# A feed-forward of seven-product block multiplications: from one fused loop to two phases through DRAM

## The chip, the core and the metric

One Trainium2 chip, one of its cores. The metric is device microseconds of one execution, lower is better. Profiles are of one execution each.

## What is computed

One layer of a hybrid decoder on 1024 tokens of width 1024, all in float32:

```python
x = layer_norm(x, emb_ln_g, emb_ln_b)
proj = x @ w_in                      # queries, keys, values, pool input
mixed = concat(stick_breaking_attention, multiscale_pool) @ w_out
x = layer_norm(ALPHA * x + mixed, ln1_g, ln1_b)
h = square(relu(x @ w_up)) @ w_down  # 1024 -> 4096 -> 1024
x = layer_norm(ALPHA * x + h, ln2_g, ln2_b)
x = layer_norm(ALPHA * x + (p @ w_ple) * sigmoid(x @ w_gate), ln3_g, ln3_b)
```

The change is in the feed-forward, the line of `h`, and in what hands its inputs over.

## The kernel before

Float32 products are made of reduced-precision ones: `split` (L59) takes a tile into a rounded part h (a ScalarE copy, L61) and the rest l (a subtraction on VectorE or POOL, L62), and `mm3` (L64 to L67) issues three matmuls, h x h, l x h and h x l, of 128 x 128 stationary by 512 moving columns. All transfers go through one queue, that of SyncE (SP), by `load` (L69), which serves for loads and stores alike.

Tiles come from pools with a fixed number of buffers for each tag (L50: "X" 16, "K" 14, "ra" 6, "at" 4, "VS" 3, "DG" 1, "wr" 2, "wt" 4, of 1024 columns each); PSUM has four tags b0, b2, b4, b6 of two banks each. The framework orders the instructions of each engine by a planned timeline, in which a buffer must be free before its next tile is written. Where a `manual_schedule` names an engine, the instructions of the block keep the order of the code on that engine.

**Up to the feed-forward.** Eight token tiles of 128 are normalised and transposed (`norm0`, L162), attention and pooling run head by head (L515 to L543), their results lie in DRAM (mspill) and the normalised input too (xspill). The output projection (L580 to L607) goes in three rounds of three, three and two token tiles; in each the eight k blocks of w_out are loaded and split, and all six (or four) banks accumulate. Eight tiles xres are loaded from xspill ahead of the first round (L566 to L568). After a round each of its tiles is added (L599), normalised (L601), transposed and split into x1h and x1l (L603 to L607).

**The feed-forward** works on 16 groups of 256 hidden columns. `up` (L635) makes a 128 x 512 block of the hidden values, one of four for a group (two halves of the hidden columns by two halves of the tokens), with 8 x 3 matmuls, then relu on ScalarE (L646) and the square on VectorE (L647). The second product takes the group's hidden values as a 2 x 2 block matrix a, and the group's rows of w_down as a 2 x 2 block matrix b. In place of eight block products it makes seven, p1 to p7, of sums and differences of the blocks (s1 to s4 of a on VectorE, t1 to t4 of b on POOL, L631, L632), each split again; some products are added up in a PSUM bank one after the other and every state of a bank is added to xres by VectorE as it is (`into`, L692, mostly L695). `down` (L708) issues three matmuls for a product and a token tile. The loop at L766 to L777 interleaves the up products of group g + 1 with the down products of group g; the last group is made plainly, with eight block products (`plain`, L727).

**The tail** (L835 to L871) has the orders of TensorE and VectorE, and at first of POOL, written out by hand: plain products, the second layer norm of tile 0 and 1 (`norm2`), then for each token tile the gate product (`gate`, L817, 48 matmuls), its merge and the third norm. The weights of the gate are split into gw ahead of it (L790 to L796).

## Time and profile before

| | us |
|---|---|
| median of 3 runs | 1269.9 (1268.44 to 1271.51) |
| the profiled execution | 1269.56 |
| its span, first to last instruction | 1267.8 |

The engines are PE (TensorE matmuls), PEld (its weight loads, beside them), DVE (VectorE), ACT (ScalarE), POOL (GpSimd) and SP (the queue of transfers). L62 is line 62 of the kernel. Matmuls overlap, so a busy PE is not one at its peak: the distance from start to start counts. "[1.92 <-DVE xres L695]" behind an instruction says that its engine stood idle for 1.92 us before it and that this VectorE instruction ended the wait. PEclk is the clock granted to TensorE, as a share of the full one.

### The profile page before, as it was taken

The page shows a single profiled execution, that of the slowest core. Times are in us where ns is not written, and L with a number is a line of the kernel's source. Part 1 is how long each engine was busy: PE and PEld are TensorE (multiplying, and loading weights), DVE is VectorE, ACT ScalarE, POOL GpSimd, SP SyncE. Part 2 cuts the span into 40 slices and gives each one's busy share as a digit, 9 for nine tenths or more (in the row PEclk, how much of TensorE's full clock was granted, in tenths as well). Part 3 has the DMA queues.
Part 4 walks back from the last instruction along what each step waited for, and adds up shares of the span by engine and source line. Part 5 has one row for each costly group of instructions (what it writes and reads, how often), then busy time and mean ns, then how long its engine had stood idle before and what let it go on. Part 6 is the DMA issues. An engine that isn't in the chain of part 4 may idle for free.

```text
span 1267.8 us, 15286 instructions
## 1 busy us (share of the span) xinstructions
PE 1204.0 (95%) x5700; PEld 997.0 (79%) x5700; DVE 991.3 (78%) x1314; ACT 476.9 (38%) x894; POOL 588.2 (46%) x429
## 2 busy tenths in 40 slices
...
GB/s 349 285 116 117 43 42 58 43 64 53 72 172 215 128 116 133 67 67 17 67 50 67 36 48 67 50 67 17 67 50 67 36 48 67 51 166 17 67 81 69
DMA packets 79802, 108.21 MB, mean 85 GB/s; under 512 B 4592, under 2 KB 59376, under 8 KB 79728
## 3 DMA queue, kind: packets, MB, share of 16 engines
...
## 4 chain that ended last, share of the span: by engine, by line
PE 70%; DVE 11%; issue 4%; POOL 3%; ACT 3%; DMA 2%; DVEq 0%; SPq 0%; POOLq 0%; ACTq 0%
PE pu L66 9%; PE pu L67 9%; PE pu L65 9%; PE pd L65 7%; PE pd L66 7%; PE pd L67 7%; PE pq L65 2%; PE pq L66 2%; PE pq L67 2%; PE tp L115 2%; PE acc L66 2%; PE o L422 2%; DVE xres L106 2%; PE acc L65 2%; PE acc L67 2%
## 5 line engine op out<-in xcount | busy, mean ns | idle before, releaser
L695 DVE TENSOR_TENSOR xres<-xres,pd 128x512 f32<-128x512 f32 x420 | 267.1, 677 | 81.0 <-PE pd L67 81.0
L66 PE MATMUL pu<-x1l,wh 128*128 128x512 f32 x512 | 199.1, 389 | 1.1 <-DVE x1l L62 1.1
L65 PE MATMUL pu<-x1h,wh 128*128 128x512 f32 x512 | 199.1, 389 | 0.9 <-DVE xres L599 0.9
L67 PE MATMUL pu<-x1h,wl 128*128 128x512 f32 x512 | 199.1, 389 | 0.0
L62 POOL TENSOR_TENSOR wl<-wraw,wh 128x1024 fp32r<-128x1024 f32 x43 | 104.7, 2437 | 189.1 <-ACT wh L61 188.3
L62 POOL TENSOR_TENSOR t<-b,t 128x512 fp32r<-128x512 f32 x63 | 86.6, 1375 | 160.4 <-ACT t L61 160.4
L61 ACT CAST wh<-wraw 128x1024 fp32r<-128x1024 f32 x68 | 71.7, 1054 | 189.1 <-PE pu L66 124.6
L66 PEld LDWEIGHTS pu<-x1l,wh 128*128 128x128 f32 x512 | 96.1, 188 | 21.5 <-DVE x1l L62 1.6
L65 PEld LDWEIGHTS pu<-x1h,wh 128*128 128x128 f32 x512 | 96.0, 188 | 21.4 <-ACT x1h L61 1.5
L67 PEld LDWEIGHTS pu<-x1h,wl 128*128 128x128 f32 x512 | 96.1, 188 | 20.4 <-POOL wl L62 0.5
L647 DVE TENSOR_TENSOR a<-a 128x512 f32<-128x512 f32 x64 | 101.8, 1590 | 7.3 <-ACT a L646 7.2
L61 ACT CAST s<-a 128x512 fp32r<-128x512 f32 x62 | 38.4, 621 | 140.6 <-DVE a L632 139.0
L100 POOL TENSOR_TENSOR rs<-var,mhalf 128x1 f32<-128x1 f32 x32 | 44.7, 1400 | 94.5 <-DVE var L98 94.5
L65 PE MATMUL pq<-xh,wh 128*128 128x512 f32 x192 | 78.0, 406 | 0.9 <-DVE ul L62 0.8
L393 DVE TENSOR_TENSOR_SCAN rr<-rr,diag 128x640 f32<-128x640 f32 (+3 forms) x32 | 71.4, 2233 | 8.2 <-ACT rr L391 8.1
L396 POOL TENSOR_TENSOR aa<-aa,rr 128x639 f32<-128x639 f32 (+3 forms) x32 | 57.0, 1781 | 44.8 <-DVE rr L393 44.8
L65 PE MATMUL pd<-t,s 128*128 128x512 f32 x192 | 74.8, 390 | 2.1 <-ACT s L61 2.1
L67 PE MATMUL pq<-xh,wl 128*128 128x512 f32 x192 | 76.7, 400 | 0.0
L62 POOL TENSOR_TENSOR b<-b,b 128x512 fp32r<-128x512 f32 x46 | 72.5, 1603 | 9.1 <-ACT b L61 9.1
L66 PE MATMUL pq<-xl,wh 128*128 128x512 f32 x192 | 76.6, 399 | 0.0
L66 PE MATMUL pd<-t,s 128*128 128x512 f32 x192 | 74.7, 389 | 0.0
L632 POOL TENSOR_TENSOR b<-b,b 128x512 f32<-128x512 f32 x45 | 71.5, 1588 | 6.5 <-DMA b<-in_w_down_dram 1.7
...
## 6 DMA issues: line engine op xcount, KB each, us to landing
b<-in_w_down_dram SPq DMA_DIRECT2D x32, 512.0 KB, 3.5
wraw<-in_w_up_dram SPq DMA_DIRECT2D x32, 512.0 KB, 4.1
wraw<-in_w_out_dram SPq DMA_DIRECT2D x24, 512.0 KB, 3.4
wraw<-in_w_in_dram SPq DMA_DIRECT2D x16, 512.0 KB, 5.2
xt<-in_x_dram SPq DMA_DIRECT2D x8, 512.0 KB, 8.1
pspill<-pe SPq DMA_DIRECT2D x8, 512.0 KB, 5.4
xspill<-xn SPq DMA_DIRECT2D x8, 512.0 KB, 5.5
vspill<-vst SPq DMA_DIRECT2D x8, 512.0 KB, 3.0
```

The lines of the kernel that those rows point to most:

```text
L61: A.copy(out=h, in_=src)
L62: (eng or V).tensor_tensor(out=l, in0=src, in1=h.bitcast(F32), op=ALU.subtract)
L65: T.matmul(ps, lhsT=lh, rhs=rh, start=start, stop=False, **kw)
L66: T.matmul(ps, lhsT=lh, rhs=rl, start=False, stop=False, **kw)
L67: T.matmul(ps, lhsT=ll, rhs=rh, start=False, stop=stop, **kw)
L100: G.tensor_tensor(out=rs, in0=var, in1=mhalf[:, 0:1], op=ALU.pow)
L106: V.scalar_tensor_tensor(out=dst[:, cs], in0=dst[:, cs], scalar=rs, in1=b[:, cs], op0=ALU.mult, op1=ALU.add)
L393: V.tensor_tensor_scan(out=rr[:, 0:n][:, ::-1], data0=rr[:, 0:n][:, ::-1], data1=diag[:, S - n:S][:, ::-1], initial=0.0, op0=ALU.mult, op1 ...
L396: G.tensor_tensor(out=aa[:, 0:n - 1], in0=aa[:, 0:n - 1], in1=rr[:, 1:n], op=ALU.mult)
L632: (V if dst[0] == "a" else G).tensor_tensor(out=value[dst], in0=value[a], in1=value[b], op=op)
L647: V.tensor_tensor(out=rl, in0=rl, in1=rl, op=ALU.mult)
L695: V.tensor_tensor(out=xres[i][:, cs], in0=xres[i][:, cs], in1=src, op=ALU.add)
```

## The change

The seven-product scheme is used for the first product too, and the two products no longer alternate.

- **Phase one** makes the hidden values of all 16 groups. The 2 x 2 blocks are now those of w_up (two halves of 512 input features by the group's two halves of hidden columns, sums on VectorE, `up_first`, `up_rest`) and of the transposed x (two halves of the features by two halves of the tokens, sums t1 to t4 made once, in `second_half` and `x_sums`). A product is 4 x 3 matmuls instead of 8 x 3, and there are seven for a group instead of four. Relu and square are both on ScalarE. VectorE then makes the sums s1 to s4 for the second product, and four tiles `hid` go to DRAM (hspill, seven blocks of 512 columns a group). `down_sums` loads the rows of w_down, POOL makes their four sums in place, and four stores bring them to DRAM (tspill).
- **Phase two** takes two groups a step, in eight steps. `down_operands` reloads the blocks in four stages j (hidden values, side 0, split with VectorE; the blocks of w_down and its sums, side 1, split with POOL), and `down` adds the two groups' products (2 x 3 matmuls) in a bank before `into` takes it.
- Tag "X" has 8 buffers of twice the width (`big`). The normalised x goes to DRAM (rspill) and comes back as xres ahead of phase two; in the output projection three tiles xr are loaded ahead and one more as each is done.
- The tail's hand-written order has the last step's products, and gw 4 to 7 are made within it.

The diff, cut to its core (`tt` is a tensor_tensor, a subtraction unless it says add; `up_two` splits a tile and names its halves; `down_values` loads a stage's raw blocks):

```diff
-    BUFS = {"X": 16, "K": 14, "ra": 6, "at": 4, "VS": 3, "DG": 1, "wr": 2, "wt": 4}
+    BUFS = {"X": 8, "K": 14, "ra": 6, "at": 4, "VS": 3, "DG": 1, "wr": 2, "wt": 4}
...
+    def big(name):
+        return sb.tile([P, 2048], F32R, name=name, tag="X", bufs=BUFS["X"])
...
-            for m in range(2):
-                split(tp[:, 2 * m:2 * m + 2, :], xh[i // 4][2 * q + m][:, :, ts],
-                      xl[i // 4][2 * q + m][:, :, ts])
+            split(tp, xh[i // 4][q][:, :, ts], xl[i // 4][q][:, :, ts])
...
-        mixh[k], mixl[k] = slot("X", "mixh", F32R), slot("X", "mixl", F32R)
+        both = big("mix")
+        mixh[k], mixl[k] = both[:, 0:S], both[:, S:2 * S]
...
+    OPS = {"p1": ("a11", "b11"), "p2": ("a12", "b21"), "p3": ("s4", "b22"), "p4": ("a22", "t4"),
+           "p5": ("s1", "t1"), "p6": ("s2", "t2"), "p7": ("s3", "t3")}
...
+    def first_half(t, tps):
+        ts = slice(t * P, (t + 1) * P)
+        xval[t] = slot("ra", "xval")
+        for cs, name, tp in zip((L, R), ("b11", "b21"), tps):
+            A.copy(out=xval[t][:, cs].rearrange(tokens, t=P), in_=tp)
+            x_split(name, tp, ts)
...
+    def second_half(t, tps):
+        ts = slice(t * P, (t + 1) * P)
+        t12, t34 = slot("ra" if t % 2 == 0 else "K", "t12"), slot("ra" if t % 2 == 0 else "K", "t34")
+        t1, t2, t3, t4 = t12[:, L], t12[:, R], t34[:, L], t34[:, R]
+        b11, b21 = xval[t][:, L], xval[t][:, R]
+        v = lambda u: u.rearrange(tokens, t=P)
+        tt(V, v(t1), tps[0], v(b11))
+        tt(V, v(t2), tps[1], v(t1))
+        x_split("b22", tps[1], ts)
+        tt(V, t3, t2, b11)
+        tt(V, t4, b21, t2)
+        return ts, {"t2": v(t2), "t1": v(t1), "t3": v(t3), "t4": v(t4)}
+    def x_sums(ts, vals):
+        for name in ("t2", "t1", "t3", "t4"):
+            if name not in xb:
+                xb[name] = [big(name + w).rearrange(tokens, t=CH) for w in "hl"]
+            split(vals[name], xb[name][0][:, :, ts], xb[name][1][:, :, ts])
...
+    def up_load(g, f):
+        wraw[g, f] = slot("wr" if f == 0 else "DG", "uraw")
+        load(wraw[g, f].rearrange("p (k c) -> p k c", c=P),
+             w_up[:, (2 * g + f) * P:(2 * g + f + 1) * P].rearrange("(k p) c -> p k c", p=P))
+    def up_first(g):
+        up_load(g, 0)
+        up_two(g, ("a11", "a12"), wraw[g, 0], "wt" if g == 1 else "at")
+    def up_rest(g):
+        up_load(g, 1)
+        r1, r2 = wraw[g, 0], wraw[g, 1]
+        s21 = slot("VS", "s21")
+        tt(V, s21[:, R], r2[:, L], r2[:, R], ALU.add)
+        tt(V, s21[:, L], s21[:, R], r1[:, L])
+        up_two(g, ("s2", "s1"), s21, "wt")
+        tt(V, r2[:, L], r1[:, L], r2[:, L])
+        up_two(g, ("s3", "a22"), r2, "wt")
+        tt(V, r1[:, R], r1[:, R], s21[:, L])
+        both = slot("VS", "s4", F32R)
+        split(r1[:, R], both[:, L], both[:, R])
+        wop[g, "s4"] = both[:, L], both[:, R]
...
+    hspill = dram.tile([NG, P, 7 * CH], F32, name="hspill")
+    tspill = dram.tile([NG, P, 4 * CH], F32, name="tspill")
+    rspill = dram.tile([NT, P, D], F32, name="rspill")
+    def down_sums(g):
+        r = [slot("K", "draw") for _ in range(2)]
+        for f in range(2):
+            load(r[f], w_down[(2 * g + f) * P:(2 * g + f + 1) * P, :])
+        tt(G, r[0][:, L], r[0][:, R], r[0][:, L])
+        tt(G, r[0][:, R], r[1][:, R], r[0][:, R])
+        tt(G, r[1][:, R], r[1][:, R], r[0][:, L])
+        tt(G, r[1][:, L], r[1][:, L], r[1][:, R])
+        for n, (f, cs) in enumerate(((1, R), (0, L), (0, R), (1, L))):
+            load(tspill[g, :, n * CH:(n + 1) * CH], r[f][:, cs])
...
+    def up(g, name):
+        a, b = OPS[name]
+        wh, wl = wop[g, a]
...
+        for k in range(4):
+            xh1, xl1 = x_op(b, k)
+            ks = slice(k * P, (k + 1) * P)
+            mm3(ps, wh[:, ks], wl[:, ks], xh1, xl1, first and k == 0, True,
+                skip_group_check=not first or k > 0)
+        a11, a12 = hidden(g, 0)[:, L], hidden(g, 0)[:, R]
+        if name == "p1":
+            A.copy(out=a11, in_=ps)
+        if name == "p2":
+            tt(V, a11, ps, a11, ALU.add)
+            relu2(a11)
+        if name in ("p6", "p7", "p4", "p3"):
+            a22, a21 = hidden(g, 3)[:, L], hidden(g, 3)[:, R]
+        if name == "p6":
+            A.copy(out=a21, in_=ps)
+        if name == "p7":
+            A.copy(out=a22, in_=ps)
+            tt(V, a22, ups[g, "B"], a22, ALU.add)
+            relu2(a22)
+        if name == "p4":
+            relu2(a12, ps)
+            load(hspill[g, :, 0:2 * CH], hidden(g, 0))
+            load(hspill[g, :, 6 * CH:7 * CH], a22)
+        if name == "p3":
+            tt(V, a21, ps, a21, ALU.add)
+            relu2(a21)
+            s2, s1 = hidden(g, 1)[:, L], hidden(g, 1)[:, R]
+            s4, s3 = hidden(g, 2)[:, L], hidden(g, 2)[:, R]
+            tt(V, s1, a21, a22, ALU.add)
+            tt(V, s2, s1, a11)
+            load(hspill[g, :, 2 * CH:4 * CH], hidden(g, 1))
+            tt(V, s4, a12, s2)
+            tt(V, s3, a11, a21)
+            load(hspill[g, :, 4 * CH:6 * CH], hidden(g, 2))
...
+    for i in range(3):
+        xr[i] = slot("at", "xr")
+        load(xr[i], xspill[i])
...
+            up_first(0)
+            for w in waiting:
+                x_sums(*w)
+            up_first(1)
...
+            tps = [transposed(xr[i], "b6", 4 * q, 4) for q in range(2)]
+            if i < 4:
+                first_half(i, tps)
+            else:
+                w = second_half(i - 4, tps)
+                if i < 6:
+                    waiting.append(w)
+                else:
+                    x_sums(*w)
+            load(rspill[i], xr[i])
+            if i + 3 < NT:
+                xr[i + 3] = slot("at", "xr")
+                load(xr[i + 3], xspill[i + 3])
+    with tc.manual_schedule(engines={mybir.EngineType.PE}):
+        for g in range(2):
+            up(g, "p1")
+            up(g, "p2")
+        up_rest(0)
+        for g in range(NG):
+            down_sums(g)
+            if 2 <= g + 1 < NG:
+                up_first(g + 1)
+            up(g, "p6")
+            up(g, "p5")
+            up(g, "p7")
+            if g + 1 < NG:
+                if g:
+                    up(g + 1, "p1")
+                    up(g + 1, "p2")
+                up_rest(g + 1)
+            up(g, "p4")
+            up(g, "p3")
...
+    xtags = ["DG", "VS", "VS", "VS", "ra", "ra", "ra", "ra"]
+    xres = [slot(xtags[i], f"xres{i}") for i in range(NT)]
+    for i in range(NT):
+        load(xres[i], rspill[i])
+    stages = (("p1", "p2"), ("p6", "p5"), ("p3", "p7"), ("p4",))
+    raws = ((("at", "at"), ("wr", "wr")), (("at", "at"), ("ra", "ra")),
+            (("wt", "wt"), ("K", "K")), (("wt", "wt"), ("wt", "wt")))
...
+    def down_values(g, j, side, raw):
+        if side == 0:
+            load(raw[:, 0:CH if j == 3 else S], hspill[g, :, j * S:min(j * S + S, 7 * CH)])
+            return
+        w1, w2 = [w_down[(2 * g + f) * P:(2 * g + f + 1) * P, :] for f in range(2)]
+        tsp = [tspill[g, :, n * CH:(n + 1) * CH] for n in range(4)]
+        if j == 1:
+            load(raw, tspill[g, :, 0:2 * CH])
+        else:
+            for cs, src in zip((L, R), ((w1[:, L], w2[:, L]), None, (w2[:, R], tsp[2]),
+                                        (tsp[3],))[j]):
+                load(raw[:, cs], src)
...
+    def down_operands(s, j):
+        for q in range(2):
+            g = 2 * s + q
+            for side in range(2):
+                raw = slot(raws[j][q][side], "draw%d" % j)
+                down_values(g, j, side, raw)
+                if j == 3:
+                    both = slot("K", "dop", F32R)
+                    h, l, raw = both[:, L], both[:, R], raw[:, L]
+                elif j == 2:
+                    h, l = slot("K", "doph", F32R), slot("K", "dopl", F32R)
+                else:
+                    both = big("dop")
+                    h, l = both[:, 0:S], both[:, S:2 * S]
+                split(raw, h, l, (V, G)[side])
...
+    def down(s, name, t):
+        a, b = OPS[name]
+        ts = slice(t * P, (t + 1) * P)
         first = name in ("p1", "p5", "p2")
...
+        for q in range(2):
+            (ah, al), (bh, bl) = dop[2 * s + q, a], dop[2 * s + q, b]
+            mm3(ps, ah[:, ts], al[:, ts], bh, bl, first and q == 0, True,
+                skip_group_check=not first or q > 0)
+        r, c = takers[name]
         into(r, t, c, ps)
...
+    PART1 = [("p1", t) for t in range(4)]
+    PART2 = [(name, t) for t in range(4) for name in ("p2", "p6")]
+    PART3 = [("p5", 0), ("p5", 1), ("p7", 0), ("p3", 0), ("p7", 1), ("p3", 1),
+             ("p5", 2), ("p5", 3), ("p7", 2), ("p3", 2), ("p7", 3), ("p3", 3)]
+    PART4 = [("p4", t) for t in range(4)]
+    for j in range(4):
+        down_operands(0, j)
+    NS = NG // 2
+    with tc.manual_schedule(engines={mybir.EngineType.PE}):
+        for s in range(NS - 1):
+            for part, js in ((PART1, ()), (PART2, (0,)), (PART3, (1, 2)), (PART4, (3,))):
+                for name, t in part:
+                    down(s, name, t)
+                for j in js:
+                    down_operands(s + 1, j)
...
+        for name, t in PART1 + PART2:
+            down(NS - 1, name, t)
+        for k in range(4, NK):
+            gate_weights(k)
+        g3 = load_rows("K", ln3_g[0], "g3")
+        b3 = load_rows("K", ln3_b[0], "b3")
         with tc.manual_schedule(engines={mybir.EngineType.Pool}):
-            plain(0)
-            plain(1)
+            gate_rest(4)
+            gate_rest(5)
+            for name, t in PART3[0:4]:
+                down(NS - 1, name, t)
             norm2(0)
-            for k in (6, 7):
-                gate_rest(k)
-            for i in range(2, 5):
-                plain(i)
+            gate_rest(6)
+            for name, t in PART3[4:]:
+                down(NS - 1, name, t)
+            gate_rest(7)
+            tps = turn2(0)
+            rest2(0, tps)
+            for name, t in PART4[0:2]:
+                down(NS - 1, name, t)
             norm2(1)
-        tps = turn2(0)
-        rest2(0, tps)
-        for i in range(5, NT):
-            plain(i)
+        for name, t in PART4[2:]:
...
+            down(NS - 1, name, t)
```

## Rows read from the trace of the kernel before

**Rows 1.** The page, part 1: busy us, share of the span, instructions.

```profile
PE 1204.0 (95%) x5700; PEld 997.0 (79%) x5700; DVE 991.3 (78%) x1314; ACT 476.9 (38%) x894; POOL 588.2 (46%) x429
```

**Rows 2.** Stages: start:end, length, busy PE PEld DVE ACT POOL; PEclk, DMA share, GB/s.

```profile
368.30:388.70 20.40, 8.97 (x45) 7.73 (x44) 5.30 (x9) 5.73 (x9) 6.05 (x3) 0.64 0.94 357
388.70:491.00 102.30, 98.49 (x432) 79.48 (x432) 70.36 (x91) 38.30 (x53) 38.45 (x18) 0.96 0.38 128
491.00:533.70 42.70, 38.43 (x170) 30.30 (x171) 35.53 (x46) 16.95 (x31) 27.08 (x17) 1.00 0.34 101
533.70:1130.00 596.30, 596.30 (x2632) 493.75 (x2632) 497.48 (x628) 184.85 (x293) 313.25 (x190) 1.00 0.18 55
1157.60:1268.00 110.40, 97.98 (x488) 81.09 (x488) 90.92 (x127) 17.11 (x32) 38.44 (x28) 0.97 0.17 62
```

**Rows 3.** Groups by line, TensorE (tiles, shapes, count | busy us, mean ns | idle).

```profile
L67 PE MATMUL pu<-x1h,wl 128*128 128x512 f32 x512 | 199.1, 389 | 0.0
```

**Rows 4.** Timeline, TensorE, start of the feed-forward (start, us, instruction, [idle before <-releaser]).

```profile
509.18 0.50 PE L66 MATMUL pu<-x1l,wh 128*128 128x512 f32 x1 [1.14 <-DVE x1l L62]
...
529.30 0.50 PE L65 MATMUL pd<-t,s 128*128 128x512 f32 x1 [2.14 <-ACT s L61]
```

**Rows 5.** Groups by line on VectorE, ScalarE and POOL.

```profile
L695 DVE TENSOR_TENSOR xres<-xres,pd 128x512 f32<-128x512 f32 x420 | 267.1, 677 | 81.0 <-PE pd L67 81.0
...
L62 POOL TENSOR_TENSOR wl<-wraw,wh 128x1024 fp32r<-128x1024 f32 x43 | 104.7, 2437 | 189.1 <-ACT wh L61 188.3 <-PE acc L67 0.8
...
L647 DVE TENSOR_TENSOR a<-a 128x512 f32<-128x512 f32 x64 | 101.8, 1590 | 7.3 <-ACT a L646 7.2
...
L61 ACT CAST wh<-wraw 128x1024 fp32r<-128x1024 f32 x68 | 71.7, 1054 | 189.1 <-PE pu L66 124.6 <-PE acc L66 33.4 <-DMA wraw<-in_w_out_dram 10.4
...
L632 POOL TENSOR_TENSOR b<-b,b 128x512 f32<-128x512 f32 x45 | 71.5, 1588 | 6.5 <-DMA b<-in_w_down_dram 1.7 <-PE pd L66 1.2 <-PE pd L67 0.2
...
L646 ACT ACTIVATE a<-pu 128x512 f32<-128x512 f32 x64 | 38.0, 594 | 21.2 <-PE pu L67 21.1
...
L62 DVE TENSOR_TENSOR wl<-wraw,wh 128x1024 fp32r<-128x1024 f32 x25 | 32.1, 1284 | 22.3 <-ACT wh L61 20.4 <-PE acc L67 1.1 <-DMA xres<-xspill 0.7
```

**Rows 6.** Timeline, VectorE, POOL idle (first row) and busy (second).

```profile
498.39 0.68 DVE L647 TENSOR_TENSOR a<-a 128x512 f32<-128x512 f32 x1
...
503.09 1.78 DVE L647 TENSOR_TENSOR a<-a 128x512 f32<-128x512 f32 x1
```

**Rows 7.** DMA issues, whole span (tiles, queue, count, KB each, us to landing).

```profile
b<-in_w_down_dram SPq DMA_DIRECT2D x32, 512.0 KB, 3.5
...
out_dram<-xres SPq DMA_DIRECT2D x7, 512.0 KB, 2.9
mraw<-mspill SPq DMA_DIRECT2D x6, 512.0 KB, 10.2
```

**Rows 8.** DMA view of 368 to 392 us.

```profile
DMA packets 2362, 8.64 MB, mean 360 GB/s; under 512 B 253, under 2 KB 253, under 8 KB 2362
```

**Rows 9.** Timeline, SP's queue, TensorE and ScalarE, start of the output projection.

```profile
370.16 3.04 SPq L70 DMA_DIRECT2D xres<-xspill  x5
...
377.38 6.70 SPq L70 DMA_DIRECT2D mraw<-mspill  x6
...
382.03 1.97 PE L453 MATMUL pb<-ident,ms 128*128 128x128 f32 x8 [4.67 <-POOL ms L446]
388.71 0.80 PE L65 MATMUL acc<-wh,mixh 128*128 128x512 f32 x1 [4.71 <-ACT mixh L61]
...
387.61 1.04 ACT L61 CAST mixh<-mraw 128x1024 fp32r<-128x1024 f32 x1 [9.94 <-DMA mraw<-mspill]
```

**Rows 10.** Timeline, VectorE's norm2(0), then TensorE at the first gate.

```profile
1139.61 1.27 DVE L94 BATCH_NORM_STATS2 st<-xres 128x6 f32<-128x512 f32 x2
...
1142.95 3.42 DVE L106 SCALAR_TENSOR_TENSOR xres<-xres,rs,b 128x1024 f32<-128x1024 f32 x1 [0.45 <-POOL rs L100]
...
1157.64 0.47 PE L65 MATMUL pg<-gwh,x2h 128*128 128x512 f32 x1 [1.92 <-DVE xres L695]
```

246 lines of the change are left out of this document (75 added, 171 removed).

## The prediction

> **What bounds the kernel now.** The page's busy shares come first: TensorE is at 95%, VectorE second at 78% [rows 1]. Such shares are averages, so the next view is the table by stages [rows 2]. Between 533.7 and 1130 us, where the feed-forward runs group after group, TensorE is busy for all 596.30 of 596.30 us at a granted clock of 1.00 (the 2.4 GHz level), VectorE for 497.48, POOL for 313.25. So there nothing but the number of matmuls counts: 2632 are recorded, 596.30 / 2632 = 0.2266 us each (start to start; the 389 ns of a row overlap). Two stages are otherwise. From 368.3 to 388.7, ahead of the output projection, TensorE works 8.97 of 20.40 us while the DMA engines are 94% busy. In the last 110.40 us VectorE works 90.92 and TensorE 97.98: both wait for each other there.
>
> The sum is made against the profiled execution's own 1269.56 us; the median of the runs, 1269.9, is 0.3 us above that, so the answer holds for it too. 0.2%, some 2.5 us, is what a measurement can tell from no change.
>
> **Matmuls removed.** Before, the first product has 16 groups x 4 blocks x 8 x 3 = 1536 matmuls (512 on each of three lines [rows 3]); the second 15 x 7 x 4 x 3 + 96 = 1356. After, each up product has only four k blocks: 16 x 7 x 4 x 3 = 1344; the down products 8 steps x 7 x 4 x 2 x 3 = 1344. 2892 become 2688: 204 x 0.2266 = **-46.2 us**, if TensorE stays the bound. Phase one then has 84 x 0.2266 = 19.0 us a group, phase two 168 x 0.2266 = 38.1 us a step. The rest asks what could break these periods.
>
> **Phase one, VectorE and ScalarE.** A group needs on VectorE three subtractions of 1024 columns, nine of 512 with both inputs in SBUF, and three of 512 that read PSUM. Alone a 512 one takes 0.68, next to a busy POOL 1.78 [rows 6]; one of 1024 takes 1.28 [rows 5]. Sum alone: 3.9 + 6.1 + 2.0 = 12.0 us. POOL's four sums (4 x 1.59 = 6.4 us [rows 5]) can cost VectorE no more than they last: 18.4 at the worst, under 19.0. ScalarE: 3 x 1.05 and twelve of some 0.6 [rows 5]: 10.4 us. Hidden, cost 0; without that cover each us over 19.0 costs 16.
>
> **Phase one, DMA.** A group moves 1.05 MB of w_up, 1.05 of w_down, 1.05 of its sums out and 1.84 of hidden values out: 5.0 MB in 19.0 us, 262 GB/s. While the queue never ran dry the chip moved 360 GB/s on average [rows 8]. So the engines are some 73% busy against 18% now [rows 2]: enough, with longer landings. All goes through SP's one queue, in a fixed order, 12 transfers a group where it had four. The slowest loop in it is down_sums: two buffers of tag K are loaded, POOL makes four sums in place, four stores must land before the next load. Lower bound 3.5 (load) + 6.4 + 2.9 (store) = 12.8 us; upper 10.2 + 6.4 + 10.2 = 26.8 with landings as in the saturated stretch [rows 7]. At 73% I take the side of the free landings, 16 to 18 us, under 19.0; single late loads cost **+3 us** (0 to +124, the last being 7.8 x 16).
>
> **Start of the output projection.** Before, SP issues eight loads of xres ahead of the reloads of mspill; the first mix split waits 9.94 us for its reload and the first projection matmul starts at 388.71, while the transposes before it ended at 384.0 [rows 9]. After, only three xr loads and no w_down load stand there: 2.6 + 0.5 MB less, 8.7 us at 360 GB/s [rows 8], more than the 4.7 us of waiting. The next thing late is those transposes, on the rms chain. **-5 us** (-9, if the projection also goes ahead of them, to 0).
>
> **Start of the feed-forward.** Before, TensorE stands idle 42.70 - 38.43 = 4.3 us in the stretch after 491 [rows 2], 1.14 and 2.14 of them in two waits for operands [rows 4]. After, 48 matmuls of p1 and p2 of two groups need the first four token tiles alone and cover 10.9 us, as 48 did before. But p6 wants t2 of the last token tile: on VectorE t1, t2, b22, t3, t4 and four splits for tiles 6 and 7, about 2 x 9 x 0.65 = 12 us in place of 3, and up_rest's operands, some 6 us; the squares (1.59 each [rows 5]) go to ScalarE. I add **+5 us** (0 to +12, if none of the added 15 is hidden by more than the old waits).
>
> **Seam between the phases.** Step 0 needs values of groups 0 and 1, stored some 270 us earlier; four of the eight big buffers come free with p5 of group 15, three products (8.2 us) before TensorE runs dry, and a split takes 1.05 + 1.28 or 2.44 [rows 5]. A store must land for the last rows of xres, but their first use is late. No row shows such a seam; the nearest is the 4.7 us wait at 388.71 [rows 9]. **+3 us** (0 to +10).
>
> **Phase two.** A step has on VectorE 28 additions of a bank x 0.677 = 19.0 (56 before for the same two groups: the gain of two blocks per bank, which lies under TensorE and is worth nothing by itself), six splits of 1024 and two of 512: 28.0 us alone. Its splits meet POOL's, six x 2.44 + 2 x 1.4 = 17.4 us. The mean square of before took 1.59 in place of 0.68 [rows 5, 6], 0.9 lost beside POOL's 512-column ops; scaled to POOL's 2.44, 1.4 for each 1024: 28.0 + 6 x 1.4 + 2 x 0.9 = 38.2 against TensorE's 38.1. That is the row with the greatest loss, so VectorE stays just below; local waits, where an addition stands behind a slow split and p3 or p5 wants its bank, **+5 us**. The loss can be no more than POOL's own 17.4 us a step, 45.4 in all, 7.3 x 8 = 58 us: the range is 0 to +58. Its 20 loads bring 7.3 MB a step, 193 GB/s or 54% of what the queue can do: each stage is loaded a stage or more ahead, cost 0.
>
> By the Trainium skill (SBUF — State Buffer, Who interferes with whom), a VectorE instruction with two SBUF inputs and a GpSimd one that reads SBUF exclude each other, and the second to start waits until the first is through. By that rule, with each of the eight splits caught from POOL's first cycle, the upper end above would be the answer. The rows agree in kind, 0.68 against 1.78 [rows 6]; that each is caught is not what the mean of 1.59 shows.
>
> **The tail.** In the last step norm2(0) stands in VectorE's order ahead of the additions of p7 and p3 of t = 1. It lasts 6.8 us (1139.61 to 1146.37 [rows 10]), while TensorE has 18 matmuls (4.1 us) before p5 of t = 3 wants a bank: some 4 us of wait. norm2(1) stands ahead of the additions of the last two p4, whose banks the first gate product takes: 7.5 - 2.7 = 4.8 us against 1.92 now [rows 10]. **+7 us** (-2 to +10). From there the tail is as before.
>
> **Small things.** One split of 512 in place of two of 256 at the start, on a stretch that other work fills: **-1 us** (-2.5 to 0). The stores and reloads of rspill, 0.5 MB each, lie under some 100 us of projection with the DMA 38% busy [rows 2]: 0.
>
> **Sum:** -46.2 + 3 - 5 + 5 + 3 + 5 + 7 - 1 = -29.2; 1269.6 - 29.2 = 1240.4, call it **1241 us**.
>
> **Rivals.**
> A. *Slower: the down_sums loop sets the pace.* SP issues in a fixed order, so when the loop (load, four POOL sums, stores landed) takes longer than planned, the loads of w_up and the stores of hidden values behind it are late and TensorE waits in every group. For: the DMA load rises to four times, and in the only saturated stretch landings are 10.2 us [rows 7]. Against: 73% is not saturated, and w_up has a buffer ahead. It costs from 19.0 us a group on; with the 29 us won, the change is slower from 19.0 + 32 / 16 = 21.0. At 22: 1241 + 48 - 3 = 1286. Chance 0.14.
> B. *VectorE bounds phase two.* At 42 us a step, half of what POOL can take: (42 - 38.1) x 8 = 31, less the 5 counted: 1267. For: VectorE is already at 83% in the steady stretch [rows 2] and is as close after. Against: the additions halve. It decides from 38.1 a step. Chance 0.10.
> C. *Every one of VectorE's splits stands still for the whole of POOL's* beside it, 45.4 us a step: 58 less 5 more, 1294. For: both sides' splits follow ScalarE's copies at the same moment. Against: POOL is idle for half the time [rows 2]. Chance 0.04. The rule of the Trainium skill cited above (SBUF — State Buffer, Who interferes with whom), taken at its worst, gives this case.
> D. Waits at the start, seam and tail and a mild A cancel the gain: 1267 to 1273. Chance 0.04.
> That the change does not remove the matmuls is excluded: they are counted in the code.
>
> **Numbers.** My case has 0.68; its own range is 1219 (projection start -9, start and seam 0, tail -2) to 1257 (start +12, seam +10, tail +10). Taking in B and the mild end of A, 1220 to 1278 leaves out some 0.18. Faster by over 0.2%: 0.68, B's larger part 0.08, A's mild end 0.02, so 0.78; the same 0.04; slower 0.18.
>
> **What the profile after will show.** TensorE matmuls at 0.227 us start to start in both phases, with no gaps longer than 1 us inside a group; phase one 302 us, phase two 302 us. The first projection matmul at about 384. Waits at p6 of group 0 (some 5 us), at p5 of t = 3 in the last step (4) and at the first gate (5). I am wrong on phase one if the waits ahead of up products end on a DMA or on a w_up split and the period of a group is over 20; wrong on phase two if TensorE's waits there end on VectorE's additions and sum to more than 15 us; wrong on the matmuls if their spacing differs from 0.227.

## The result, and the profile of the changed kernel

The changed kernel takes 1348.51 us (1343.23 to 1349.68, four runs) against 1269.59 before on the same chip: 1.0612 times as long, interval 1.058 to 1.0643. It is slower, by 79 us, where 29 us less were forecast. The profiled execution took 1347.72 us, with a span of 1345.9. The engines' busy times (page of the profile, part 1):

```profile
PE 1190.3 (88%) x5496; PEld 967.0 (72%) x5496; DVE 941.5 (70%) x1181; ACT 559.9 (42%) x948; POOL 512.0 (38%) x356
```

TensorE fell from 95% [rows 1] to 88%: the matmuls went, but it waits. Where, the table of stretches tells (start:end, length, busy PE, PEld, DVE, ACT, POOL, granted clock, DMA share, GB/s); the stretches are the projection, the start of the feed-forward, phase one with the loop of down_sums and behind it, the seam, phase two, and the gate:

```profile
388.70:490.00 101.30, 95.13 (x429) 76.07 (x429) 76.24 (x97) 42.27 (x62) 36.64 (x17) 0.99 0.47 165
490.00:535.70 45.70, 27.79 (x101) 20.80 (x99) 39.42 (x61) 18.54 (x30) 7.92 (x6) 0.74 0.32 107
560.00:760.00 200.00, 172.89 (x714) 137.28 (x715) 120.76 (x126) 85.00 (x131) 76.63 (x52) 0.96 0.78 257
785.00:865.00 80.00, 79.28 (x350) 65.31 (x350) 49.64 (x62) 45.27 (x66) 6.16 (x3) 1.00 0.62 208
872.00:905.00 33.00, 11.76 (x39) 8.82 (x40) 16.85 (x16) 8.52 (x12) 9.90 (x5) 0.65 0.91 344
920.00:1160.00 240.00, 225.50 (x966) 179.25 (x965) 177.88 (x207) 80.66 (x92) 115.33 (x46) 1.00 0.53 177
1234.80:1345.90 111.10, 98.83 (x488) 81.85 (x488) 89.75 (x125) 17.10 (x32) 38.33 (x28) 0.96 0.17 62
```

Before, TensorE was busy for all of the feed-forward's steady stretch [rows 2]. Now it is so only from 785 to 865, where GpSimd has finished the loop. In phase one ScalarE's copy of p7 out of PSUM (line 709) marks each group: the first starts at 535.75, the eleventh at 770.29, the sixteenth at 862.81. The ten groups up to 770 take 23.5 us each in the mean (the first has 60 matmuls, the others 84), where 19.0 were forecast for 84. TensorE's waits there, and ScalarE's (us in total, times, longest; 560 to 760):

```profile
PE pu L69 <- ACT hid L709: 16.1, 8, 4.8
PE pu L69 <- ACT hid L707: 14.8, 7, 3.2
```
```profile
ACT uh L65 <- DVE s L567: 53.7, 8, 8.1
ACT uh L65 <- DMA uraw<-in_w_up_dram: 21.7, 8, 3.4
```

TensorE waits for PSUM banks that ScalarE copies out late, and ScalarE has time for them: it works 85 of 200 us. But it takes its instructions in a fixed order, and ahead of those copies stand casts of w_up that wait for a load, or for VectorE's sum of a load. One group, from the timelines (start, us, engine, instruction, [idle before <- releaser]):

```profile
640.71 1.23 DVE L66 TENSOR_TENSOR ul<-uraw,uh 128x1024 fp32r<-128x1024 f32 x1 [0.91 <-ACT uh L65]
642.22 0.43 SPq L74 DMA_DIRECT2D uraw<-in_w_up_dram  x1
647.84 0.69 DVE L567 TENSOR_TENSOR s<-uraw 128x512 f32<-128x512 f32 x1 [2.01 <-DMA uraw<-in_w_up_dram]
649.82 1.05 ACT L65 CAST uh<-s 128x1024 fp32r<-128x1024 f32 x1 [5.49 <-DVE s L567]
651.35 1.77 DVE L567 TENSOR_TENSOR uraw<-uraw,s 128x512 f32<-128x512 f32 x1
653.16 0.62 ACT L65 CAST s<-uraw 128x512 fp32r<-128x512 f32 x1 [2.29 <-DVE uraw L567]
653.68 0.58 ACT L709 COPY hid<-pu 128x512 f32<-128x512 f32 x1
654.32 0.50 PE L69 MATMUL pu<-t4h,uh 128*128 128x512 f32 x1 [1.48 <-ACT hid L709]
655.25 0.68 DVE L66 TENSOR_TENSOR s<-uraw,s 128x512 fp32r<-128x512 f32 x1
655.96 0.38 SPq L74 DMA_DIRECT2D uraw<-in_w_up_dram  x1
660.63 1.05 ACT L65 CAST uh<-uraw 128x1024 fp32r<-128x1024 f32 x1 [2.29 <-DMA uraw<-in_w_up_dram]
662.78 1.04 ACT L65 CAST uh<-uraw 128x1024 fp32r<-128x1024 f32 x1
663.85 1.33 DVE L66 TENSOR_TENSOR ul<-uraw,uh 128x1024 fp32r<-128x1024 f32 x1 [0.91 <-ACT uh L65]
668.00 0.39 SPq L74 DMA_DIRECT2D uraw<-in_w_up_dram  x1
```

The load of the second rows goes out as the split before lets go of their one buffer (642.22) and is summed at 647.84, 5.6 us later. The cast behind it holds ScalarE for 5.49 us, the next one for 2.29 (VectorE's sums take 1.77 beside GpSimd), and only then comes the copy that TensorE wants.

The seam, TensorE and ScalarE:

```profile
872.72 0.50 PE L69 MATMUL pd<-dop 128*128 128x512 f32 x1 [0.79 <-DVE hid L567]
895.41 0.80 PE L69 MATMUL pd<-dop 128*128 128x512 f32 x1 [16.23 <-ACT dop L65]
900.49 0.79 PE L70 MATMUL pd<-dop 128*128 128x512 f32 x1 [4.29 <-POOL dop L66]
```
```profile
890.34 1.04 ACT L65 CAST doph<-draw 128x1024 fp32r<-128x1024 f32 x1 [12.38 <-DMA draw<-tspill]
891.29 4.07 ACT L65 CAST dop<-draw 128x512 fp32r<-128x512 f32 x6
```

The same pattern: a cast of the third stage waits 12.38 us for its load, and behind it stand the casts of the second, which TensorE wants. DMA moves 344 GB/s there; stores of hidden values, five of the eight loads of xres (they go out from 874 to 883) and step 0's operands meet.

In phase two a step takes 41.8 us (from 916.41 to 1167.06 in six). VectorE's additions stand among its splits, and many of these are stretched beside GpSimd's (groups of 930 to 1160):

```profile
L849 DVE TENSOR_TENSOR xres<-xres,pd 128x512 f32<-128x512 f32 x150 | 96.6, 680 | 22.6 <-PE pd L71 22.6
L66 DVE TENSOR_TENSOR dop<-draw,dop 128x1024 fp32r<-128x1024 f32 x20 | 40.6, 2028 | 0.0
```

The 2028 ns are the mean of two kinds: ten of the twenty splits take 1.22 us, the other ten 2.83 to 2.84. TensorE waits for the additions (930 to 1190):

```profile
PE pd L69 <- DVE xres L849: 14.5, 21, 1.3
```

The longest of these waits, six of 1.14 to 1.35 us and 7.7 us in all, end on additions behind a split that is not stretched but late. One of them:

```profile
941.77 2.43 DVE L66 TENSOR_TENSOR dop<-draw,dop 128x512 fp32r<-128x512 f32 x1 [1.16 <-issue]
944.23 0.32 SPq L74 DMA_DIRECT2D draw<-hspill  x1
947.89 1.05 ACT L65 CAST doph<-draw 128x1024 fp32r<-128x1024 f32 x1 [4.65 <-DMA draw<-hspill]
949.03 1.23 DVE L66 TENSOR_TENSOR dopl<-draw,doph 128x1024 fp32r<-128x1024 f32 x1 [1.94 <-ACT doph L65]
950.17 3.11 DVE L849 TENSOR_TENSOR xres<-xres,pd 128x512 f32<-128x512 f32 x5
950.91 0.50 PE L69 MATMUL pd<-dop 128*128 128x512 f32 x1 [1.33 <-DVE xres L849]
```

A stretched split (2.43 us for 512 columns) ends at 944.20, and the load of hspill waits for it. Its cast stands 4.65 us for the landing, VectorE 1.94 us for the cast, and the additions come after the split that follows. All six have this chain. The stretch (2.43 to 2.49 us, where the like split behind takes 1.18) is about as long as the wait, so it may be its source; that is argued, not shown.

### The profile page after: what moved, and what is told of

The parts are those of the page before. It is cut to its first block, busy times and chain, and to the rows that moved or that the text cites. A ratio compares the mean times of both kernels' runs of the same rounds, so it can differ in the third digit from the quotient of the medians.

```text
span 1345.9 us, 15487 instructions
## 1 busy us (share of the span) xinstructions
PE 1190.3 (88%) x5496; PEld 967.0 (72%) x5496; DVE 941.5 (70%) x1181; ACT 559.9 (42%) x948; POOL 512.0 (38%) x356
## 5 line engine op out<-in xcount | busy, mean ns | idle before, releaser
L66 POOL TENSOR_TENSOR dop<-draw,dop 128x1024 fp32r<-128x1024 f32 (+1 forms) x48 | 123.6, 2595 | 195.4 <-PE pd L71 101.6
L849 DVE TENSOR_TENSOR xres<-xres,pd 128x512 f32<-128x512 f32 x208 | 134.7, 680 | 43.9 <-PE pd L71 43.9
L69 PE MATMUL pd<-dop 128*128 128x512 f32 x320 | 128.9, 403 | 34.8 <-DVE xres L849 17.3
L567 POOL TENSOR_TENSOR draw<-draw 128x512 f32<-128x512 f32 x64 | 93.5, 1460 | 164.6 <-DMA draw<-in_w_down_dram 87.1
L70 PE MATMUL pd<-dop 128*128 128x512 f32 x320 | 126.4, 395 | 4.3 <-POOL dop L66 4.3
L71 PE MATMUL pd<-dop 128*128 128x512 f32 x320 | 126.1, 394 | 0.0
L65 ACT CAST dop<-draw 128x1024 fp32r<-128x1024 f32 (+1 forms) x96 | 80.0, 904 | 93.9 <-PE pd L71 92.2
L66 DVE TENSOR_TENSOR dop<-draw,dop 128x1024 fp32r<-128x1024 f32 (+1 forms) x48 | 96.6, 2018 | 17.7 <-ACT dop L65 16.5
L69 PEld LDWEIGHTS pd<-dop 128*128 128x128 f32 x320 | 60.9, 190 | 56.1 <-DVE xres L849 25.3
L66 DVE TENSOR_TENSOR ul<-uraw,uh 128x1024 fp32r<-128x1024 f32 x32 | 40.4, 1264 | 54.1 <-ACT uh L65 54.1
L70 PEld LDWEIGHTS pd<-dop 128*128 128x128 f32 x320 | 61.1, 191 | 16.9 <-POOL dop L66 4.8
L71 PEld LDWEIGHTS pd<-dop 128*128 128x128 f32 x320 | 61.0, 191 | 13.0
L66 POOL TENSOR_TENSOR dopl<-draw,doph 128x1024 fp32r<-128x1024 f32 x16 | 38.3, 2395 | 69.1 <-ACT doph L65 50.6
L66 DVE TENSOR_TENSOR atl<-tp,ath 128x512 fp32r<-128x512 f32 (+2 forms) x96 | 50.7, 546 | 15.0 <-ACT ath L65 14.3
```

What stands on the lines that cost most here:

```text
L65: A.copy(out=h, in_=src)
L66: (eng or V).tensor_tensor(out=l, in0=src, in1=h.bitcast(F32), op=ALU.subtract)
L69: T.matmul(ps, lhsT=lh, rhs=rh, start=start, stop=False, **kw)
L70: T.matmul(ps, lhsT=lh, rhs=rl, start=False, stop=False, **kw)
L71: T.matmul(ps, lhsT=ll, rhs=rh, start=False, stop=stop, **kw)
L567: eng.tensor_tensor(out=o, in0=i0, in1=i1, op=op)
```

## The experiments

All start from the changed kernel; times are beside 1269 to 1271 us for the kernel before. "Excess" is the time from the first to the last copy of p7 less 280.2 us, which 60 + 14 x 84 = 1236 matmuls take at 0.2267; the changed kernel has 327.1 - 280.2 = 46.9.

Four of the kernels were run two or four times, the others once, and a few us of difference in time say little: ahead of all these edits, the first up product starts anywhere from 484.6 to 492.8 us. The excess is steadier: in three runs below whose edits lie behind phase one (under Seam, Phase two and Together) it is 44.2, 49.6 and 47.2.

**Phase one: what the loop costs.** No loop, phase two reading w_down in its place:

```diff
-            down_sums(g)
```


> The loop of down_sums is left out, and phase two reads rows of w_down where it would read the sums. If that loop is the whole of what phase one lost (ten groups of 23.4 us against 18.5 behind it), every group takes 18.5 to 19 us, phase one lasts 300 to 310 us from the end of the projection's tail on, and the run takes 1290 to 1300. If ScalarE's casts wait ahead of the PSUM copies whatever GpSimd does, groups stay above 21 us and the run above 1325.

1296.91 us (1295.95 to 1297.86); excess 1.9. TensorE is busy throughout:

```profile
560.00:760.00 200.00, 200.00 (x884) 165.58 (x884) 118.60 (x160) 105.83 (x156) 0.00 (x0) 1.00 0.46 154
```

So the loop accounts for 45 of the 46.9 us. (An earlier execution of the same kernel took 1696 us at a granted clock of 0.64 to 0.67 in every stretch, and is not compared.) With loads and stores kept and the four sums left out:

```diff
-        tt(G, r[0][:, L], r[0][:, R], r[0][:, L])
...
```


> Leaves out POOL's four sums of a group; the rows of w_down are loaded and stored as they are, so bytes, transfers and their order of dependence stay. If the length of the loop load, POOL, store is what holds SP's queue up, it becomes 6 us shorter and a group takes 20 us or less (time 1310 to 1320). If the transfers themselves are the cost, a group still takes 22 to 24 us and the time stays near 1345.

1318.19 us, excess 15.5, with the DMA engines far busier than in the changed kernel:

```profile
560.00:680.00 120.00, 115.52 (x494) 93.74 (x493) 65.75 (x89) 58.78 (x89) 0.00 (x0) 0.98 0.95 324
```

Transfers alone thus cost some 14 us even at 95% and 324 GB/s, and 31 us hang on the sums. ScalarE stands at the head of its queue for loads and sums of w_up as much as before, 31.2 + 15.0 us in these 120 against 53.7 + 21.7 in 200, while TensorE loses little. So such standing costs only where a copy that TensorE wants comes behind it, and its total does not tell the loss. Whether contention is what the sums cost, the next run asks:

```diff
-        tt(G, r[0][:, L], r[0][:, R], r[0][:, L])
+        tt(V, r[0][:, L], r[0][:, R], r[0][:, L])
...
```


> The four sums of down_sums run on VectorE and not on GpSimd; loads, stores and everything else stay as in the changed kernel. Contention theory (GpSimd's sums stretch VectorE's two-SBUF-operand operations beside them to 0.9 to 1.8 us, which frees the one buffer of the second rows of w_up late, and the casts that stand ahead of ScalarE's PSUM copies wait for the late load): with GpSimd idle in phase one VectorE's operations go back to 0.69 us, its 4 x 0.69 = 2.8 us more a group fit into a group of 18.5 us, a group falls from 23.4 towards 19 to 20 us while the loop runs, and the run to about 1300 to 1320 us, as without the sums (1318). Rival, the transfers theory (the loop's 2.1 MB a group beside the loads of w_up are what makes these late): no gain, 1340 to 1350. Second rival, VectorE's own queue: its sums wait for the landing of the draw rows and hold up the split of w_up behind them, so that it is slower than 1348, as the PSUM copies on VectorE were (1370).

1337.48 us, excess 38.1. VectorE's sum uraw - s falls from 1363 ns to 685, so the stretching was GpSimd's:

```profile
L567 DVE TENSOR_TENSOR uraw<-uraw,s 128x512 f32<-128x512 f32 x8 | 10.9, 1363 | 0.0
```
```profile
L567 DVE TENSOR_TENSOR uraw<-uraw,s 128x512 f32<-128x512 f32 x9 | 6.2, 685 | 0.0
L567 DVE TENSOR_TENSOR draw<-draw 128x512 f32<-128x512 f32 x52 | 35.9, 690 | 40.9 <-DMA draw<-in_w_down_dram 36.0 <-issue 4.4
```

(changed kernel first, then this one). VectorE now stands 36 us for the loop's own loads, and the net gain is 9 us. What contention alone costs is not told apart: it is taken away here, but the sums stand in VectorE's queue instead.

**Phase one: whose queue.** The loop's transfers on GpSimd's queue:

```diff
-            load(r[f], w_down[(2 * g + f) * P:(2 * g + f + 1) * P, :])
+            G.dma_start(out=r[f], in_=w_down[(2 * g + f) * P:(2 * g + f + 1) * P, :])
...
```


> The loads and stores of down_sums are issued by POOL instead of SP; bytes and sums are the same. Theory queue (loads of w_up stand behind down_sums' waits in SP's fixed order): a group takes 18.5 to 19.5 us, the time is about 1300 to 1308. Rival bandwidth (the engines are 75 to 85% busy and landings are late whoever issues): still 22 us or more a group, time 1335 to 1350.

1342.32 us, excess 39.0: SyncE no longer waits for GpSimd, but for squares. The copies of p6 and p7 on VectorE:

```diff
-            A.copy(out=a21, in_=ps)
+            V.tensor_copy(out=a21, in_=ps)
...
```


> The PSUM copies of p6 and p7 are made by VectorE instead of ScalarE, nothing else. Theory ScalarE's order (TensorE waits for these copies since they stand on ScalarE behind casts of weights that wait for a load, while the weights themselves are early enough): a group takes 20 us or less while down_sums runs, the time falls by 30 us or more, to 1315 or less. Rival: the weights are late for TensorE too, so it waits for their splits instead: a group stays above 22 us, the time above 1335.

1370.19 us, excess 73: TensorE now waits 34.4 us (560 to 760) for VectorE's copies of p6. ScalarE and VectorE kept in the order of the code as TensorE is:

```diff
-    with tc.manual_schedule(engines={mybir.EngineType.PE}):
+    with tc.manual_schedule(engines={mybir.EngineType.PE, mybir.EngineType.Activation, mybir.EngineType.DVE}):
```


> In phase one ScalarE and VectorE too keep the order of the code, in which the casts of a group's weights stand behind the PSUM copies of p6 and p7 of the group before; all loads, stores and sums stay, and so does the one buffer DG. Theory fixed order (copies wait behind casts that wait for loads): with down_sums still there a group takes 18.5 to 20 us instead of 23.4, TensorE waits for no ScalarE copy for over 1 us, and the time falls by 35 to 45 us to 1303 to 1313. Rival loads (w_up itself arrives too late for TensorE) or contention with POOL's sums: a group stays above 22 us, TensorE waits for casts or subtractions of weights instead, the time above 1335.

1394.66 us, excess 99: TensorE waits 19.4 us for casts of w_up and 19.0 for copies of p6. All casts of w_up on VectorE:

```diff
-        split(val, h, l)
+        V.tensor_copy(out=h, in_=val)
+        tt(V, l, val, h.bitcast(F32))
...
```


> In phase one every rounding cast of w_up and of its sums is made by VectorE, right before the subtraction that needs it, and none by ScalarE; loads, sums and everything else stay. Head-of-line theory (ScalarE's PSUM copies of p6 and p7 are late because casts that wait for loads and for VectorE's sums, 75 us of waits in 560 to 760, stand ahead of them in its fixed order): ScalarE's waits for uraw and s go to none, TensorE's 31 us of waits for hid L707 and L709 in that stretch fall under 8, a group takes 19 to 21 us, and the run about 1300 to 1320. Rival (the weights themselves are late: load, sum, cast and subtraction take longer than a group gives them beside the loop of down_sums): TensorE then waits for ul or s in place of the copies and the run stays at 1340 or more. Second rival (VectorE, 60% busy there with operations stretched by GpSimd, gets some 4 casts of 0.7 to 1.1 us a group more and becomes the bound): TensorE waits for DVE hid, 1350 or more.

1354.17 us, excess 53. ScalarE waits for no load any more, but 105.6 us for VectorE's sums of hidden values, and TensorE waits 26.9 us for ScalarE's copies of p6. It is VectorE that waits for the loads now (560 to 760):

```profile
DVE uh L629 <- DMA uraw<-in_w_up_dram: 37.3, 9, 5.0
DVE s L567 <- DMA uraw<-in_w_up_dram: 18.7, 8, 4.0
```

So no single queue among these is the cause: the wait goes wherever the first reader of the load is put, and what stands behind it there is late. So is the load itself late?

**Phase one: the loads of w_up.** The second rows in K buffers, alone and with the loop on GpSimd's queue:

```diff
-        wraw[g, f] = slot("wr" if f == 0 else "DG", "uraw")
+        wraw[g, f] = slot("wr" if f == 0 else "K", "uraw")
```


> The second rows of w_up go into the K buffers (14, nearly all unused in phase one) in place of the single DG buffer; GpSimd's sums stay. If the single buffer is what makes the load of w_up late (it starts only when the group before has let go of it), the load can be issued a group earlier, ScalarE's casts no longer wait for it (21.7 us on the load and 53.7 us on the sum behind it in 560 to 760), TensorE's 31 us of waits for the two PSUM copies in that stretch shrink to under 10, and the run falls by 25 to 45 us, to 1305 to 1325. Rival (VectorE's stretched operations alone hold up the casts, whenever the load lands): 1335 to 1350. Second rival (the planner's order of ScalarE is worked out with its own landing times, and it will put the casts earlier as well, so that they wait again): about 1348 with the waits on the same names.

> Two edits together: the second rows of w_up go into K buffers, and the loads and stores of down_sums are issued by GpSimd, so that a load of w_up stands neither behind a GpSimd sum in SyncE's queue (67 us of waits in 560 to 760 with the K buffers alone) nor behind its own buffer (17 us in the changed kernel). Theory (each of the two alone leaves the other in the way: 1342 and 1396 us): the loads go out a group early, ScalarE no longer waits for uraw, and the run takes 1300 to 1320. Rival (the order of ScalarE's casts ahead of its PSUM copies is what costs, and the planner moves the casts up as the loads come earlier): 1335 to 1360 with TensorE still waiting for hid L707 some 25 us in 200.

1395.73 and 1409.12 us, excess 96 and 93. In the first, loads of w_up stand in SyncE's queue behind the loop's stores, which wait 67 us for GpSimd's sums; in the second behind stores of hidden values, which wait 104 us for squares. The loads issued by GpSimd (sums on VectorE), and by ScalarE (sums on GpSimd):

```diff
-        load(wraw[g, f].rearrange("p (k c) -> p k c", c=P),
+        G.dma_start(out=wraw[g, f].rearrange("p (k c) -> p k c", c=P),
...
```


> As vsums (the sums of down_sums on VectorE, 1337 us, 22.5 us a group), and GpSimd, idle there, issues the loads of w_up: these stand behind nothing but their own buffers, and no longer in SyncE's queue behind stores that wait for sums and squares. Queue theory (in the changed kernel a load of w_up goes out late because it stands in SyncE's fixed order behind stores of tspill and hspill that wait, and the late load is then waited for at the head of ScalarE's queue): VectorE's and ScalarE's waits for uraw fall to a third, TensorE's 20 us on hid L707 in 560 to 760 to under 7, a group to 19 to 20.5 us, the run to 1290 to 1310. Rival (once issued a load takes 5.6 us beside the loop's transfers, and that alone makes it late): 1325 or more, with the same waits.

> The loads of w_up are issued by ScalarE; GpSimd makes the sums as in the changed kernel. By the queue theory a load stands now in ScalarE's order, behind its waits for sums and squares but not behind GpSimd's sums (44 us of SyncE's waits in 560 to 760): part of the loss comes back, 1315 to 1335. Rival (ScalarE's queue is the one that runs late, so that the loads become later still, as in the run with the loop's transfers on GpSimd and the K buffers): 1350 or more.

1344.15 and 1348.61 us, excess 45 and 46: no gain. In the first nothing but its buffer holds up a load, and it is as late; so the buffers were the next suspect.

GpSimd's loads, VectorE's sums and the K buffers in one (the diffs above), with the three edits of the run told last:

> All that helped, and the last theory of phase one. Ring theory: in the changed kernel the two loads of w_up of a group run one after the other through two buffers. The load of the second rows goes out as the DG buffer is let go (642.22, behind VectorE's split that ended 641.94), lands 5.6 us later, sums, casts and splits end at 655.93, which lets go of the buffer of the first rows; their next load goes out at 655.96, lands at 660.6, its cast stands ahead of the cast of the second rows in ScalarE's queue, that one's split ends at 665.2, and the next load of the second rows goes out at 668.00: 25.8 us round. Without the loop's transfers and GpSimd the same ring is 18.5 us (799.02 to 817.48). So no one of the queue, the contention and the buffer alone brings it down, and all three must go together: here GpSimd issues the loads of w_up (no queue), VectorE makes the sums (no contention), and the second rows use K buffers (no ring). Beside them the splits on GpSimd, the loads of xres behind the first stages and the turned tail, as in the run of these three together (1299 us). Expected: a group at 19 to 20 us while the loop runs (84 matmuls at 0.2267 us are 19.04), 10 x 3.5 to 4.4 us = 35 to 44 less than 1299: 1255 to 1265, about as fast as the kernel before or a little faster. Rival (with the K buffers the planner again orders casts ahead of loads, as in the two other runs with them): groups of 23 us or more and 1300 to 1340 in all.

1329.57 us (ratio 1.0463, 1.0445 to 1.0482), excess 71, and 30 us more than the three edits take without the rest. Its loads waited for VectorE's splits and, by way of the K buffers, for stores (GpSimd, 560 to 760):

```profile
POOL uraw L624 <- DVE s L66: 106.1, 9, 12.9
POOL uraw L624 <- DMA tspill<-draw: 50.5, 5, 12.6
POOL uraw L624 <- DMA hspill<-hid: 26.6, 3, 12.0
```

```diff
-        wraw[g, f] = slot("wr" if f == 0 else "K", "uraw")
+        wraw[g, f] = slot("wr" if f == 0 else "VS", "uraw")
-        s21 = slot("VS", "s21")
+        s21 = slot("DG", "s21")
```


> As ring_cut, except for the buffers: there the second rows of w_up in K buffers waited for stores of the loop that had held the same buffers (GpSimd's loads stood 50 us for a landing of tspill and 27 us for one of hspill in 560 to 760), so that the ring was closed again by way of the loop, and 1330 us says nothing against the ring. Here the second rows use the three VS buffers in turn with s4, and s21 has the DG buffer: a load of them goes out when the last product of the group before the last has read s4, a whole group ahead, and waits for no transfer of the loop. Ring theory: a group takes 19 to 20.5 us while the loop runs, TensorE's waits for hid and ul in 560 to 760 are under 10 us in all, and the run takes 1255 to 1270. Rival (the planner puts the casts ahead of the landings again, wherever the load stands, because it counts on shorter landings than the 6.3 us here): a group of 21.5 us or more, 1285 or more, with waits for ACT hid L707.

1309.88 us (ratio 1.0313, 1.0287 to 1.0339), excess 58, again more than the three edits alone (1299.41, told last). Here the loads do come early; the sum at 650.86 waits for none of them. It waits for its turn on VectorE:

```profile
643.93 0.69 DVE L567 TENSOR_TENSOR draw<-draw 128x512 f32<-128x512 f32 x1 [1.86 <-DMA draw<-in_w_down_dram]
647.24 0.69 DVE L567 TENSOR_TENSOR draw<-draw 128x512 f32<-128x512 f32 x1 [2.62 <-DMA draw<-in_w_down_dram]
...
650.86 0.69 DVE L567 TENSOR_TENSOR s<-uraw 128x512 f32<-128x512 f32 x1
```

and ScalarE's cast at 652.84 has stood 8.97 us for it. The ring theory, that two loads in series set the period, fails as the sole cause: with the ring cut a group still takes 24 us (532.88 to 774.39 in ten), now behind the loop's loads.

**Start.** x_sums' subtractions on GpSimd:

```diff
-            split(vals[name], xb[name][0][:, :, ts], xb[name][1][:, :, ts])
+            split(vals[name], xb[name][0][:, :, ts], xb[name][1][:, :, ts], G)
```


> The subtractions of the splits of t1 to t4 go from VectorE to POOL, which is idle at the start of the feed-forward. Theory VectorE bounds the start (it is busy for all 20 of 20 us from 500 to 520): 16 x 0.65 = 10 us leave it, POOL takes 1.4 each beside it; p6 of group 0, now at 522, starts at 512 to 516 and the time falls by 6 to 10 us. Rival: the layer norm of tiles 6 and 7 and their transposes set it: p6 still at 520 or later, time within 3 us of 1348.

1346.71 us, within the changed kernel's own 1343.23 to 1349.68. From the first up product to the first copy of p7 it takes 48.3 us where it took 45.9: VectorE's part shrinks, and TensorE waits longer for VectorE's sums t ahead of its transposes (4.32 us for 2.49) and for ScalarE's t2h (6.47 for 5.30).

**Seam.** The loads of xres behind the first two stages of step 0:

```diff
-    for i in range(NT):
-        load(xres[i], rspill[i])
...
+    down_operands(0, 0)
+    down_operands(0, 1)
+    for i in range(NT):
+        load(xres[i], rspill[i])
...
```


> The eight loads of xres are issued behind those of the first two stages of step 0. Theory transfers at the seam (xres fills the queue ahead of the operands of p6): TensorE's gap of 16.2 + 4.3 us between the phases falls below 8 us, the time to about 1333. Rival order on ScalarE (casts of later stages stand ahead of the stage that is needed): the gap stays above 15 us.

1332.64 us, 16 less. Not all of it is the edit's: the feed-forward, from the first up product to the first gate product, takes 733.8 us for 745.0, 11 less, and the gap 10.3 us for 20.5, which is more than the 8 expected:

```profile
882.68 0.79 PE L69 MATMUL pd<-dop 128*128 128x512 f32 x1 [8.69 <-ACT dop L65]
885.10 0.79 PE L70 MATMUL pd<-dop 128*128 128x512 f32 x1 [1.63 <-POOL dop L66]
```

**Phase two.** GpSimd subtracts both sides' splits:

```diff
-                split(raw, h, l, (V, G)[side])
+                split(raw, h, l, G)
```


> In phase two both sides' splits are subtracted by POOL, so VectorE has only its 28 additions a step, each with one input in PSUM. Theory port (a VectorE subtraction beside a POOL one takes 2.0 instead of 1.2 us and the additions behind it are late): TensorE's waits for additions vanish and a step takes 38 us or less instead of 41.8, if POOL's 34 us keep up; time about 1320 to 1330. Rival: VectorE's additions alone set it, or POOL is too slow: a step takes 41 us or more, the time stays or rises.

1326.58 us, 22 less; the feed-forward takes 731.6 us, 13 less, though the seam grew to 20.9 + 7.1 us of waits. From 930 to 1190 TensorE waits for nothing. So VectorE's splits among its additions were the cost of the steady steps. Whether by their stretching beside GpSimd or by the operands that they stood for is not told apart: the edit takes both away.

**Together**: that edit from the second step on, the loads of xres moved, and in the last step the turning and norms later:

```diff
+                split(raw, h, l, G if s else (V, G)[side])
...
-            tps = turn2(0)
-            rest2(0, tps)
             for name, t in PART4[0:2]:
                 down(NS - 1, name, t)
-            norm2(1)
-        for name, t in PART4[2:]:
-            down(NS - 1, name, t)
+            tps = turn2(0)
+            rest2(0, tps)
+            for name, t in PART4[2:]:
+                down(NS - 1, name, t)
+            norm2(1)
...
```


> Three edits together. GpSimd subtracts both sides' splits in phase two from the second step on; the loads of xres stand behind the first two stages of the first step; at the end the fourth part of the last products is turned and the gate's first norm comes later. Shares if they add up: seam 16, splits 22 less what GpSimd's extra splits cost at the seam there (its gap was 28 us, this form keeps the old split in the first step, so that up to 8 more come back), tail 0 to 4. Main theory: 1300 to 1312. If the two gains overlap (the seam's shorter gap only brings the splits of phase two together): 1320 to 1330.

1299.41 us (1296.15 to 1303.98), ratio 1.0237 (1.0202 to 1.0271); 49 us less than the change, 42 of them in the feed-forward (703.3 us). Phase two is at its bound, with GpSimd the busiest beside TensorE:

```profile
920.00:1160.00 240.00, 240.00 (x1061) 198.79 (x1060) 121.52 (x177) 90.68 (x105) 212.15 (x103) 1.00 0.58 189
```

Its phase one still has an excess of 47 us (533.10 to 860.51). Without that it would take an estimated 1252, less than the kernel before: a subtraction, not a run. No version that was run beats the kernel before.

## Why the prediction was wrong, step by step

The whole of the feed-forward, from the first up product to the first gate product, took 666.6 us before and 745.0 after (489.89 to 1234.85), the rest 0.2 us less. By the terms of the sum, in us:

| term | forecast | measured | from |
|---|---|---|---|
| matmuls | -46.2 | -46.2 | spacing 0.2267, as forecast |
| phase one | +3 | +50.4 | 46.9, and 3.5 behind the last copy |
| start of the projection | -5 | -1.1 | first up product 489.89 for 491.04 |
| start of the feed-forward | +5 | +17.5 | 45.9 to the first copy, less 84 matmuls (19.0), less 9.4 before (666.6 - 655.3 - 1.9) |
| seam | +3 | +21.7 | 16.2 + 4.3 + 0.8 + 0.4 |
| phase two | +5 | +28.9 | the rest of 871.78 to 1231.55 over 1344 matmuls: 3.6 a step |
| tail | +7 | +6.8 | 4.5, 3.3 - 1.9 and 0.9 |
| small | -1 | 0 | |

**Matmuls**: right, and so was the reason that TensorE would be the bound in a group without waits (19.0 us in the run without the loop).

**Phase one**, the step that failed most: "*16 to 18 us, under 19.0; single late loads cost +3 us*". The loop did run at about the pace forecast: 52 stores in 200 us are 13 rounds, 15.4 us each. That a loop quicker than a group costs nothing was the error. Nothing holds it to one round a group either: its 16 rounds fall on the first ten groups (sums from 529.6 to 764). Rival A named the right part (the loop; slower from 21 us a group, measured 23.5) with a narrower path than the one found: taking the loop's transfers off SyncE's queue gains a net 8 us (excess 39.0). The sign named for phase one came by half: the period is over 20, but TensorE's waits end on ScalarE's copies and not on loads or splits. Shown is that the loop costs 45 us, that its transfers alone cost 14, and that another engine for the casts, the copies, the loop's transfers, the sums or the loads gains 9 us at the most. By which path the other 31 come stays open. That the planner's order, made with other landing times than these 5 to 6 us, ties all queues into one another is argued, not shown: the run with the order of the code on ScalarE and VectorE was slower still (excess 99), and none had an order planned with these times. "*18.4 at the worst, under 19.0*" added up VectorE's work right (120.76 us in 200, 60%) but a sum says nothing on the order in which it comes.

**Start of the projection**: the wait behind xres was gone as forecast, acc at 386.53 straight behind the transposes; but these came 2.4 us later themselves, and the end of the projection gained 1.1. With 484.6 to 492.8 in the other profiles, this term is not known to better than a few us.

**Start of the feed-forward**: the place was right ("*p6 wants t2 of the last token tile*"), the size not:

```profile
515.49 1.11 PE L119 MATMUL tp<-ident,xr 128*128 128x128 f32 x4 [2.49 <-DVE t L567]
521.90 0.80 PE L69 MATMUL pu<-t2h,uh 128*128 128x512 f32 x1 [5.30 <-ACT t2h L65]
524.90 0.80 PE L70 MATMUL pu<-t2l,uh 128*128 128x512 f32 x1 [2.20 <-DVE t2l L66]
```

VectorE is busy for all of 490 to 520, and the granted clock of 490 to 535.7 is 0.74 in the mean, between the level of 1.2 GHz (0.5) and the full one, after 0.99 in the projection: TensorE works 27.79 of 45.70 us there, and some of the matmuls that do run start 0.43 us apart in place of 0.2267 (from 492.66 to 496.09, and from 525.49 to 529.76). That is some 4 of the 17.5 us. I had given the whole +15 as hidden but 5; the range's end of +12 was nearer.

**Seam**: "*+3 us (0 to +10)*" came from a row of another place and thought of buffers and splits. What was missed is order: xres loads ahead of step 0's operands cost 10 of the 21.7 (the run that moves them), and the rest of the gap stays. What makes the rest was not tried.

**Phase two**: the mechanism forecast, additions behind slow splits, is a part of what was found. In the six longest waits, 7.7 of 14.5 us, the split ahead is late and not slow: its load goes out only as a slow split before it ends. So "*each stage is loaded a stage or more ahead, cost 0*" failed too: the load of 944.23 goes out 5 us ahead of its split. VectorE at 74% (177.88 of 240, 31 us a step for the 38.2 summed) is not the bound, so rival B holds in its time (42 us a step for 41.8) and not in its reason. Of the 28.9, some 2.5 are matmuls behind the seam's gap, 0.43 us apart from 901.08 to 905.35 at a granted clock of 0.50 (the 1.2 GHz level).

By the Trainium skill (SBUF — State Buffer, Who interferes with whom), a VectorE instruction with at most one input in SBUF does not contend with GpSimd, outside the two-port perf modes, and one with two contends with a GpSimd instruction that reads SBUF. The trace agrees: additions that read PSUM take 673 to 689 ns where GpSimd's split covers them, and ten splits beside GpSimd's take 2.83 to 2.84 us where those that meet none take 1226 ns. Rival C, every split held for the whole of GpSimd's, would be 45.4 us a step, and did not come: the other ten take 1.22 us.

**Tail**: right in the waits named (4.51 at p5 of t = 3 for the 4 forecast, 3.30 at the gate for 4.8). That the sum comes to 6.8 for 7 is in part luck, as 0.9 of it lies behind the first gate product, where nothing was forecast.
